# Self-attention in a hybrid decoder step: the sums of all query blocks' squares in one run of column-group passes

## The chip, the cores and the metric

The kernel runs on one core of one Trainium2 chip. The metric is the device time of one execution in microseconds. The kernel before was timed at 1400.28, 1399.35 and 1399.48 us, a median of 1399.48 us. Lower is better.

## The reference, cut to what matters

One layer of a decoder computes, for 256 prompt tokens and 8 sample tokens, a combined input projection, sliding-window attention beside a state-space (SSD) mixer, an output projection, cross-attention into 256 memory tokens, and a gated feed-forward part. The change lies in the attention of the prompt, where each of the 16 heads of 64 numbers is normed by its own root mean square:

```python
def rms_norm(x, g):
    xf = x.astype(jnp.float32)
    y = xf * lax.rsqrt(jnp.mean(xf * xf, axis=-1, keepdims=True) + EPS)
    return (y * g.astype(jnp.float32)).astype(x.dtype)
...
    proj = rms_norm(x, w['g_mix']) @ w['w_in']
    q, k, v, z, xbc, dt_raw = jnp.split(proj, IN_SPLITS, axis=-1)
    q = rms_norm(q.reshape(b, t, N_HEADS, HEAD_DIM), w['q_norm_g'])
    k = rms_norm(k.reshape(b, t, N_KV_HEADS, HEAD_DIM), w['k_norm_g'])
```

So for every token and head the kernel needs the sum of 64 squares of the query. The kernel does not scale the queries; it applies the resulting factor to the scores, before the softmax.

## The kernel before, in words

Features lie on the 128 partitions and tokens along the free axis. Every weight matrix is streamed from memory in pieces of 128x1024 (`wraw`). ScalarE rounds a piece to a high part (`whi`, L85) and VectorE subtracts it from the original to get a low part (`wlo`, L86). TensorE then makes three passes for each product: high by high (L100), high by low activations (L101), low by high (L102). A pair of output blocks fills two PSUM banks; when it is complete VectorE takes it out with the norm factor of the token (`attn` at L409 for the queries, `u` at L734 for the convolution's inputs). Everything else that TensorE does, such as transposes, scores, sums across partitions and the SSD products, is put between these projection passes. All of it stands in one queue of TensorE that is worked off in order. The tile framework's scheduler sets the order of all engines when the kernel is built, out of the order of the code and its own estimates. `tc.issue_after(x)` adds the condition that what is issued inside comes after instruction x; `tc.high_priority()` moves work ahead.

The queries are eight blocks (j = 0 to 7) of 128 features, two heads in each, in the tile `qT` (in the trace `attn`). As each pair of blocks is ready ScalarE squares it into `qsq[j // 4]` (L611). Eight float32 matmuls (L615) then add up the squares by head. The stationary operand `nw[:, d, :]` is 32 columns wide, with two columns of ones for the two heads at places 2d and 2d + 1; it lies in the tile `zz`. Block j of half d writes to the 32 partitions from 32 j of one bank `pq` (in the trace `s`), so that the four j use the four column groups of 32 of the array, and the two halves d add into the same place. The trace shows each float32 matmul as two passes, so these are 16 passes. VectorE copies the bank to `qn` (L628), TensorE transposes it (two transposes, L278, to the tile `x`), ScalarE takes the root (L634) and VectorE the reciprocal (L635). The factors `rqs` and `nrqs` enter the softmax of `attn_first` and `attn_prompt`.

The scores of the first 128 tokens are L570, those of the second L529 and L530; the transposes of the probabilities are L278 to the tile `t`; their products with the values are L597 and L559. The SSD part that follows uses L798 (`s`), L825 (`y`, eight matmuls of 64 columns, or 16 passes), L833 and L841.

Of the kernel before, what the change touches and what calls it, by code (L numbers as in the profile page):

```python
# [16 lines left out]
TP, TS = 256, 8  # L17
# [30 lines left out]
def hybrid_decoder_step_kernel(ctx: ExitStack, tc: tile.TileContext, I, O):  # L48
    nc = tc.nc
    V, S, P, PE = nc.vector, nc.scalar, nc.gpsimd, nc.tensor  # L50
# [9 lines left out]
    def psum(tag):  # L60
        return ps.tile([128, 512], F32, tag=tag, name=tag, bufs=banks[tag])

    def T3(pool, n, dt=F32, tag=None, name=None, bufs=None):
        return pool.tile([128, n, T], dt, tag=tag, name=name or tag, bufs=bufs)
# [536 lines left out]
    qsq = [T3(apool, 4, tag="R", name=f"qsq{i}", bufs=4) for i in range(2)]  # L601
    nw = zz[:, :, 512:544]
# [7 lines left out]

            S.activation(out=qsq[j // 4][:, j % 4, :TP], in_=qT[:, j, :TP], func=AF.Square)  # L611
    pq = psum("s")
    for d in range(2):
        for j in range(4):
            PE.matmul(pq[32 * j:32 * j + 32, 0:TP], nw[:, d, :], qsq[d][:, j, :TP], start=d == 0, stop=d == 1)  # L615
    cpc = mp.tile([128, 24, 8], F32, name="cpc")
    ctmp = mp.tile([128, 2, TP], F32, tag="c", name="ctmp", bufs=2).rearrange("p a b -> p (a b)")[:, :192].rearrange("p (a b) -> p a b", b=8)

# [10 lines left out]
    pq = psum("x")  # L629
# [30 lines left out]
    for j in range(8):  # L660
        if j % 4 == 0:
            second_chunk(j // 4)
        d = 2 * (j // 4)
# [893 lines left out]
def build(shapes):  # L1557

    import concourse.bacc as bacc

    nc = bacc.Bacc("TRN2", target_bir_lowering=False, num_devices=1)
    ins = {n: nc.dram_tensor(f"in_{n}_dram", s, dt, kind="ExternalInput").ap() for n, (s, dt) in shapes.items()}
    outs = {n: nc.dram_tensor(f"out_{n}_dram", s, F32, kind="ExternalOutput").ap() for n, s in _OUTS}
    with tile.TileContext(nc, schedule_with_timeline_sim=True) as tc:
        hybrid_decoder_step_kernel(tc, ins, outs)
    return nc
# [10 lines left out]
```

## Time and profile before

| what | value |
|---|---|
| median of 3 runs | 1399.48 us |
| the profiled execution's own time | 1399.1 us |
| its span, first to last instruction | 1396.8 us |
| TensorE busy | 1391.8 us of the span |
| VectorE busy | 1051.1 us |
| ScalarE busy | 769.2 us |
| DMA queue of the weights | 60.9% of 16 engines |

The profiled execution lies 0.38 us under the median; 2.3 us of it lie outside the span. In the views, "PE" is TensorE, "DVE" VectorE, "ACT" ScalarE. A row of the chain of waits has a start, the time that this piece added to the chain, the engine, the tile written and the line, and a count of passes. A row of the timeline has start, duration, engine, line, operation and tiles; a matmul's duration there contains the time in which the next one already runs, so differences of starts are used for matmuls. A bracket at the end of a row is idle time before it and what ended it.

### The profile page before, as it was taken

The numbers are of one execution on the slowest core, as the hardware profiler recorded it, in microseconds if no ns is written. First come the engines' busy times: TensorE is split into PE (matmuls) and PEld (weight loads), VectorE is DVE, ScalarE is ACT, GpSimd is POOL, SyncE is SP. The second block draws the span as 40 slices with busy tenths as digits, with TensorE's granted clock in tenths as the row PEclk, the third lists the DMA queues.
The fourth block names the chain that finished last, engine by engine and source line by source line (L and its number), as shares of the span: only waits on it lengthen the run. The fifth ranks groups of instructions, "written<-read, shape, count | busy, mean of one in ns | idle before, by whom it ended". The sixth has DMA issues, their size and how long they took to land.

```text
span 1396.8 us, 29012 instructions
## 1 busy us (share of the span) xinstructions
PE 1391.8 (100%) x11535; PEld 1366.9 (98%) x11535; DVE 1051.1 (75%) x1874; ACT 769.2 (55%) x1255; POOL 95.9 (7%) x286
## 2 busy tenths in 40 slices
PE   9999999999999999999999999999999999999999
PEld 8999999999999999899999999999999999999998
DVE  8879799999997774578777775777577757765654
ACT  7667756556545554566565544554455445543532
POOL 0000011121010000002010000000000000000000
PEclk9999999999999999999999999999999999999999
DMA  7954477777776577675676765676566656655654
GB/s 302 321 162 137 137 218 245 231 242 249 244 220 236 182 240 264 206 249 187 190 254 216 253 210 187 212 248 217 183 212 240 196 183 197 196 181 182 191 184 138
DMA packets 89479, 298.33 MB, mean 214 GB/s; under 512 B 12032, under 2 KB 17152, under 8 KB 88832
## 3 DMA queue, kind: packets, MB, share of 16 engines
q1 hardware_dynamic: 83696, 277.35, 60.9%
q0 software_dynamic: 5504, 18.88, 4.1%
q8 instruction: 90, 1.47, 0.4%
q14 instruction: 45, 0.37, 0.1%
q10 hardware_dynamic: 144, 0.26, 0.1%
HBM read 280.77 MB, written 16.23 MB: 213 GB/s over the span
## 4 chain that ended last, share of the span: by engine, by line
PE 99%; DMA 0%; ACT 0%; DVE 0%; issue 0%
PE mm L100 21%; PE mm L101 21%; PE mm L102 21%; PE t L100 10%; PE t L102 10%; PE t L101 10%; PE t L240 1%; PE y L825 1%; PE t L278 1%; PE y L841 0%; PE mm L240 0%; PE s L240 0%; PE x L278 0%; PE t L559 0%; PE x L1137 0%; DMA open<-in_open_x_dram 0%
## 5 line engine op out<-in xcount | busy, mean ns | idle before, releaser
L85 ACT CAST whi<-wraw 128x1024 fp32r<-128x1024 f32 x440 | 459.7, 1048 | 527.4 <-PE mm L101 277.7
L86 DVE TENSOR_TENSOR wlo<-wraw,whi 128x1024 fp32r<-128x1024 f32 x440 | 540.1, 1229 | 220.6 <-ACT whi L85 216.7
L100 PE MATMUL mm<-x2h,whi 128*128 128x264 f32 x704 | 199.9, 284 | 0.0
L100 PE MATMUL t<-x2h,whi 128*128 128x264 f32 x704 | 199.8, 284 | 0.0
L102 PE MATMUL t<-x2h,wlo 128*128 128x264 f32 x704 | 199.7, 284 | 0.0
L101 PE MATMUL mm<-x2l,whi 128*128 128x264 f32 x704 | 199.6, 284 | 0.0
L101 PE MATMUL t<-x2l,whi 128*128 128x264 f32 x704 | 199.5, 283 | 0.0
L102 PE MATMUL mm<-x2h,wlo 128*128 128x264 f32 x704 | 199.4, 283 | 0.0
L101 PE MATMUL mm<-hl,whi 128*128 128x264 f32 x704 | 198.7, 283 | 0.0
L102 PE MATMUL mm<-hh,wlo 128*128 128x264 f32 x704 | 198.2, 283 | 0.0
L100 PE MATMUL mm<-hh,whi 128*128 128x264 f32 x704 | 197.2, 284 | 0.0
L100 PE MATMUL mm<-xh,whi 128*128 128x264 f32 x576 | 164.7, 287 | 0.0
L101 PE MATMUL mm<-xl,whi 128*128 128x264 f32 x576 | 164.5, 287 | 0.0
L102 PE MATMUL mm<-xh,wlo 128*128 128x264 f32 x576 | 162.8, 287 | 0.0
L101 PEld LDWEIGHTS mm<-x2l,whi 128*128 128x128 f32 x704 | 132.5, 188 | 0.0
L101 PEld LDWEIGHTS t<-x2l,whi 128*128 128x128 f32 x704 | 132.5, 188 | 0.0
L100 PEld LDWEIGHTS t<-x2h,whi 128*128 128x128 f32 x704 | 132.5, 188 | 0.0
L100 PEld LDWEIGHTS mm<-x2h,whi 128*128 128x128 f32 x704 | 132.4, 188 | 0.1
L101 PEld LDWEIGHTS mm<-hl,whi 128*128 128x128 f32 x704 | 132.4, 188 | 0.0
L102 PEld LDWEIGHTS t<-x2h,wlo 128*128 128x128 f32 x704 | 132.2, 188 | 0.0
L102 PEld LDWEIGHTS mm<-x2h,wlo 128*128 128x128 f32 x704 | 132.1, 188 | 0.0
L102 PEld LDWEIGHTS mm<-hh,wlo 128*128 128x128 f32 x704 | 131.9, 188 | 0.0
(506 smaller groups left out, 2951.5 us busy)
## 6 DMA issues: line engine op xcount, KB each, us to landing
wraw<-in_w_up_dram SPq DMA_DIRECT2D x176, 512.0 KB, 4.4
wraw<-in_w_in_dram SPq DMA_DIRECT2D x96, 512.0 KB, 4.7
wraw<-in_w_dn_dram SPq DMA_DIRECT2D x88, 512.0 KB, 4.2
wraw<-in_w_out_dram SPq DMA_DIRECT2D x48, 512.0 KB, 4.3
h<-in_h_dram POOLq DMA_DIRECT2D x32, 256.0 KB, 4.7
hn<-in_h_dram SPq DMA_DIRECT2D x16, 512.0 KB, 5.0
out_state_s_dram<-hn POOLq DMA_DIRECT2D x16, 512.0 KB, 3.8
e<-dram_la SPq DMA_DIRECT2D x16, 256.0 KB, 5.1
```

The source lines that it names most:

```text
L85: S.copy(out=hi, in_=x)
L86: V.tensor_tensor(out=lo, in0=x, in1=hi.bitcast(F32), op=ALU.subtract)
L100: PE.matmul(out, wh, xh, start=start, stop=False)
L101: PE.matmul(out, wh, xl, start=False, stop=False)
L102: return PE.matmul(out, wl, xh, start=False, stop=stop)
L240: PE.matmul(first[c][:, :T], pre[k // 2][i][:, k % 2, c * 128:(c + 1) * 128], A[k // 8][x][:, k % 8, :], start=k + i + x == 0, stop=k == K ...
L278: return PE.transpose(out, in_, cst[0:k, C_ID:C_ID + k])
L825: PE.matmul(y[o:o + 64, (h // 2) * 128:(h // 2) * 128 + 128], xdt[:, h, :], es[h // 4][:, h % 4, :], start=True, stop=True)
```

## The change

The eight sums become calls of a small function. The last block of the second half, d = 1 and j = 3, is called first, and all seven others are held behind it by `issue_after`. The order of the halves is turned round: d = 1 now starts the sum and d = 0 ends it. The eight matmuls, their operands and their result are the same.

```diff
     pq = psum("s")
-    for d in range(2):
-        for j in range(4):
-            PE.matmul(pq[32 * j:32 * j + 32, 0:TP], nw[:, d, :], qsq[d][:, j, :TP], start=d == 0, stop=d == 1)
+
+    def q_sums(d, j):
+        return PE.matmul(pq[32 * j:32 * j + 32, 0:TP], nw[:, d, :], qsq[d][:, j, :TP], start=d == 1, stop=d == 0)
+
+
+    with tc.issue_after(q_sums(1, 3).ins):
+        for d in (1, 0):
+            for j in range(4 if d == 0 else 3):
+                q_sums(d, j)
     cpc = mp.tile([128, 24, 8], F32, name="cpc")
```

The scheduler makes a new order out of this. On TensorE the sums stood in three places; this is the queue before (`qsq_676` is the half d = 0, `qsq_677` is d = 1, `mm` a bank of the projection):

```order
L102 MATMUL mm<-xh_76,wlo 128x264
L615 MATMUL s<-qsq_676,zz 32x256 x4
L615 MATMUL s<-qsq_677,zz 32x256 x2
L100 MATMUL mm<-xh_74,whi 128x264
L101 MATMUL mm<-xl_75,whi 128x264
L102 MATMUL mm<-xh_74,wlo 128x264
L100 MATMUL mm<-xh_74,whi 128x264
L101 MATMUL mm<-xl_75,whi 128x264
L102 MATMUL mm<-xh_74,wlo 128x264
L100 MATMUL mm<-xh_74,whi 128x264
L101 MATMUL mm<-xl_75,whi 128x264
L615 MATMUL s<-qsq_677,zz 32x256
```

The eighth sum follows 14 projection matmuls later. Now the queue has them in one place, 33 rows of projection later than the first of them stood:

```order
L100 MATMUL mm<-xh_74,whi 128x264
L101 MATMUL mm<-xl_75,whi 128x264
L102 MATMUL mm<-xh_74,wlo 128x264
L615 MATMUL s<-qsq_677,zz 32x256 x4
L615 MATMUL s<-qsq_676,zz 32x256 x4
```

The three runs (six matmuls, one, one) have become one run of eight; the place of the last sum in the queue is about the same.

On VectorE the copy of the sums to `qn` stood right behind the low parts of the queries (`qs`):

```order
L500 COPY u_656<-x 32x256
L656 TENSOR_TENSOR qs_1094<-attn,qs_1094 64x4x128 x2
L628 COPY qn<-s 128x256
L86 TENSOR_TENSOR wlo<-wraw,whi 128x1024
L573 TENSOR_TENSOR pe<-s,cst 128x512
```

Now one subtraction of a weight piece stands ahead of it (line numbers behind the change are higher by 6: L634 is the old L628):

```order
L500 COPY u_656<-x 32x256
L662 TENSOR_TENSOR qs_1094<-attn,qs_1094 64x4x128 x2
L86 TENSOR_TENSOR wlo<-wraw,whi 128x1024
L634 COPY qn<-s 128x256
L86 TENSOR_TENSOR wlo<-wraw,whi 128x1024
```

The copy has moved behind one instruction that does not need the sums.

The new order reaches further than the sums: TensorE's queue differs in many small places up to the output projection, where the attention's and the SSD part's matmuls slide by a few to some tens of rows against the projection. One such place is the SSD product `y` (L825) of the third group's second chunk. Before, its eight matmuls were one run:

```order
L100 MATMUL t_4507<-xh0_74,whi_4517 128x264
L101 MATMUL t_4507<-xl0_75,whi_4517 128x264
L825 MATMUL y_3762<-e_3737,xdt_3758 64x128 x4
L825 MATMUL y_3762<-e_3745,xdt_3758 64x128 x4
L102 MATMUL t_4507<-xh0_74,wlo_4518 128x264
```

Now three projection matmuls stand in its middle (L831 is the old L825, L804 the old L798):

```order
L100 MATMUL t_4508<-xh0_74,whi_4511 128x264
L831 MATMUL y_3762<-e_3737,xdt_3758 64x128 x4
L102 MATMUL mm_4363<-xh1_76,wlo_4434 128x264
L100 MATMUL mm_4363<-xh1_76,whi_4433 128x264
L101 MATMUL mm_4363<-xl1_77,whi_4433 128x264
L831 MATMUL y_3762<-e_3745,xdt_3758 64x128 x4
L804 MATMUL s_3972<-CT_1574,BT_1573 128x128
```

One run of eight matmuls has become two runs of four. Of the eight such products one was in two runs before, and two are now.

## Prediction, made before the changed kernel was run

> **What bounds the kernel now.** I read the page first, its busy shares and the chain that ended last, and then TensorE's waits.
>
> ```profile
> span 1396.8 us, 29012 instructions
> ...
> PE 1391.8 (100%) x11535; PEld 1366.9 (98%) x11535; DVE 1051.1 (75%) x1874; ACT 769.2 (55%) x1255; POOL 95.9 (7%) x286
> ...
> PEclk9999999999999999999999999999999999999999
> ...
> PE 99%; DMA 0%; ACT 0%; DVE 0%; issue 0%
> ...
> PE x L201 <- DVE eps L274: 1.2, 1, 1.2
> PE t L240 <- ACT xh L161: 0.5, 1, 0.5
> ```
>
> TensorE is busy in 1391.8 of 1396.8 us, its granted clock stays in the top tenth, and 99% of the chain is its own work. The last two rows are the whole answer to the question for whom TensorE waited: 1.7 us in the kernel, both in its opening. Behind that it runs from its queue without a stop to the end. So the time is the sum of what the queue's pieces cost TensorE, and a change in that sum reaches the end in full, as long as no wait appears. The price list is the chain of waits around the sums, where the second column is what each piece added:
>
> ```profile
> 81.35 0.12 PE mm L101
> 81.47 0.12 PE mm L102
> 81.59 0.99 PE s L615 x12
> 82.58 0.32 PE mm L100
> 82.90 0.12 PE mm L101
> ...
> 83.63 0.12 PE mm L101
> 83.76 0.55 PE s L615 x2
> 84.31 0.32 PE mm L102
> 84.62 0.12 PE mm L100
> ...
> 86.20 0.12 PE mm L101
> 86.32 0.55 PE s L615 x2
> 86.87 0.32 PE mm L102
> 87.19 0.12 PE mm L100
> ```
>
> A projection pass costs 0.12 us, but the first one behind a run of sums costs 0.32. So every run pays 0.20 us on top of its own time, for the way back to the full array: 1.19 us for the twelve passes, and 0.75 us for each of the two runs of two. The three together cost 1.19 + 0.75 + 0.75 = 2.69 us. Two passes are nearly as dear as twelve, because two passes of one matmul use one column group and come one after the other.
>
> **The sums in one run.** How the price grows with the passes is in other runs of column groups, of the same 256 columns and the same width of 32:
>
> ```profile
> 551.39 0.57 PE y L1091 x8
> 551.96 0.32 PE mm L100
> ...
> 552.75 1.85 PE x L1137 x28
> ```
>
> Eight passes, four matmuls in four column groups, cost 0.57 us, no more than two passes (0.55). The four groups work at the same time. Twenty-eight passes are three and a half sets of four matmuls and cost 1.85. If a half-filled set costs as much as a full one, four sets cost 1.85 and one 0.57, and a set adds (1.85 - 0.57) / 3 = 0.43 us. Two sets then cost 0.57 + 0.43 = 1.00, which is what the twelve passes above take, one and a half sets: 0.99. So the second set is paid already, and its empty half costs nothing to fill. The sixteen passes should take 0.99 + 0.20 = 1.19 us. Lower bound: that value, since four more passes can't make it shorter. Upper bound: eight passes twice with nothing shared, 2 x (0.57 + 0.20) = 1.54. I take 1.19, the row of the same line. This part is worth 2.69 - 1.19 = 1.50 us, and 1.15 us by the upper bound.
>
> A rule speaks against this. The Trainium skill, "TensorEngine Tiling (Array Packing)", section "Performance Considerations", has an overhead of some 60 cycles on each matmul. Sixteen passes would pay it sixteen times in any order, and joining them would save nothing of it. The rows above don't show it here: six more passes in other column groups cost 0.57 - 0.55 = 0.02 us. By the rule alone the first term would be nothing instead of 1.50, and the sum would come to a loss of 0.34, the next term.
>
> **What slides along.** The order shows that the rest of the moved work is the same matmuls in other places of the same queue, so only the number and the size of the runs count. A run of full-width passes between projection passes costs no way back, for it needs no other split of the array:
>
> ```profile
> 328.01 0.22 PE s L798 x2
> 328.23 0.13 PE t L100
> ...
> 329.46 1.02 PE y L825 x16
> 330.48 0.32 PE t L102
> ...
> 372.14 0.59 PE y L825 x8
> ...
> 376.31 0.59 PE y L825 x8
> ```
>
> The pass behind L798 takes 0.13. So for the full-width pieces (L278, L529, L570, L798, L833, L841) it doesn't matter where they stand. The runs with 64 columns (L559, L597, L825) do pay the 0.20 us. Their number I counted through the new order: L559 and L597 keep one run each, L825 has one more, the split shown above. The product as one run costs 1.02 + 0.20 = 1.22 us, in two runs 2 x (0.59 + 0.20) = 1.58. I took the difference from the starts of the timeline, which have the third digit, as 0.34 us; the rounded rows here give 0.36. Lower bound of this term: nothing, if the three projection passes between the halves leave something to share; upper bound 0.36.
>
> The other engines do the same instructions as before in another order. Behind the opening TensorE waits for none of them, as the two waits above show; what they could cost is a new wait of TensorE, and that is a rival. The weights' DMAs hang on the buffers that TensorE and the splits release, and they slide with them.
>
> **The sum.** 1.50 saved and 0.34 lost make 1.16 us less. The profiled execution took 1399.1 us and would take 1397.9. It lies 0.38 us under the median of the runs, 1399.48, and I forecast the median: 1399.48 - 1.16 = 1398.3 us. By the bounds of the two terms the gain lies between 1.15 - 0.36 = 0.79 and 1.50, so 1398.0 to 1398.7. A measurement of this kernel can tell about 0.2% from no change, 2.8 us, so this is "the same" for it.
>
> **The rivals.** *The copy of the sums comes late.* VectorE now does a subtraction of a weight piece first, and the transposes of `qn` stand some 25 projection passes behind the sums, as before:
>
> ```profile
> 84.35 1.41 DVE L656 TENSOR_TENSOR qs<-attn,qs 64x512 fp32r<-64x512 f32 x2
> ...
> 86.91 0.42 DVE L628 COPY qn<-s 128x256 f32<-128x256 f32 x1 [1.16 <-PE s L615]
> 87.48 1.23 DVE L86 TENSOR_TENSOR wlo<-wraw,whi 128x1024 fp32r<-128x1024 f32 x1
> ...
> 89.83 0.38 PE L278 MATMUL x<-cst,qn 128*128 128x128 f32 x2
> ```
>
> The copy ends at 86.91 + 0.42 = 87.33, and the transposes start at 89.83: 2.50 us to spare. A subtraction ahead of it costs at most 1.23 us, and VectorE stood idle for 1.16 us there, so it may well fit into that. Even the whole 1.23 leaves 1.27 us, and TensorE doesn't wait. It would begin to wait if the copy were late by more than 2.50 us, and the change would be a loss from 2.50 + 1.16 = 3.66 us on. The same section of the skill's page on tiling says that the copy out of PSUM can become the bottleneck when column groups make TensorE faster. Here the copy has to end before a fixed place in the queue, and by these rows it does. Chance 2%, at 1400 us.
>
> *The eviction of a convolution block comes late: the kernel gets slower.* From 96 us on the attention's VectorE work lies between the subtractions and the evictions that hand a bank back to the projection, and the new order shifts it by some 3 us against these. The tightest place that I found:
>
> ```profile
> 80.00:120.00 40.00, 40.00 (x318) 36.53 (x317) 32.33 (x81) 30.37 (x73) 0.00 (x0) 1.00 0.46 137
> ...
> 200.00:240.00 40.00, 40.00 (x342) 38.89 (x341) 40.00 (x78) 20.31 (x36) 5.24 (x10) 1.00 0.78 248
> ...
> 179.33 0.43 DVE L734 TENSOR_TENSOR u<-mm,r 128x264 f32<-128x264 f32 x1
> ...
> 180.10 0.28 PE L100 MATMUL mm<-xh,whi 128*128 128x264 f32 x1
> ```
>
> In the first two rows VectorE (third pair) is busy in 32.33 of 40 us, later in all 40: work that comes late isn't caught up quickly. In the last two the eviction ends at 179.76, and the pass that needs the bank starts at 180.10, 0.34 us later. One subtraction of 1.23 us ahead of such an eviction costs TensorE 1.23 - 0.34 = 0.89 us. One of these leaves a gain of 0.27; two make 0.62 us of loss, 1400.1; three 1.51, 1401.0; five 3.29, over 0.2%. For it speaks how full VectorE is; against it that it left TensorE no wait at all in the order before, made by the same scheduler. Chance of two to four 5%, of five or more 2%.
>
> *A gap elsewhere takes the gain.* If a wait of about 1 us appears in one place, or the opening is a little longer, the time is 1399.2 to 1399.6. Nothing in the rows speaks for one place above another. Chance 10%.
>
> *Only the sums count.* If the split of L825 costs nothing, the gain is 1.50: 1398.0. Chance 8%.
>
> *More than 0.2% faster.* This takes 1.6 us beyond the sum, and TensorE has no waits that could be removed. Chance 2%. That the change doesn't do what it says is excluded by the order shown above.
>
> **How the numbers follow.** The forecast, a gain of 0.8 to 1.4, has the remaining 71%. The likeliest median is 1398.3 us. The range takes in the bounds, the cases without a gain and the scatter of the runs before (1399.35 to 1400.28): 1397.4 to 1399.8. It leaves out the losses of two late evictions and more, and gains of over 2 us. Faster by over 0.2% has 2%, slower by over 0.2% 2%, the rest is 96%.
>
> **What would show it.** In the new profile's chain of waits there should be one row of L615 with sixteen passes, at 85 to 86 us, near 0.99 us, followed by a projection pass of 0.32. The products L825 should show four rows of eight passes at 0.59 and six of sixteen at 1.02, where one was split before. TensorE's waits should stay at the two of the opening. The forecast is wrong if the row of sixteen costs 1.3 us or more, if TensorE's waits name VectorE or ScalarE between 85 and 410 us, or if the span shrinks by less than 0.8 or more than 1.6 us.

## The result, and the profile after

The changed kernel takes 1404.08 us, the median of six runs (1402.73 to 1405.7), against 1399.58 us for the kernel before in six runs beside them (1399.32 to 1400.28). The ratio is 1.0032, with an interval of 1.0022 to 1.0043. So the change costs 4.5 us, where a gain of 1.16 was forecast. The profiled execution of the changed kernel took 1402.73 us, the shortest of its six. Further down, medians and ratios leave out three executions that were far longer than all others of their kernel: 1684 and 4834 us in e6 and 5864 us in e11.

These are the page of the changed kernel and its waits of TensorE.

```profile
span 1400.7 us, 29014 instructions
...
PE 1392.5 (99%) x11535; PEld 1367.8 (98%) x11535; DVE 1053.3 (75%) x1874; ACT 767.8 (55%) x1255; POOL 91.5 (7%) x286
...
PE 95%; DVE 3%; issue 1%; DMA 1%; ACT 0%; SPq 0%; DVEq 0%
```

```profile
PE y L831 <- ACT hp L849: 3.4, 1, 3.4
...
PE t L100 <- DVE u L896: 0.2, 1, 0.2
```

The span has grown from 1396.8 to 1400.7 us. TensorE is busy for nearly as long as before (1392.5 against 1391.8 us), but it has a wait that it did not have: 3.4 us, once, at the SSD product L831 (the old L825), for ScalarE's copy L849 (the old L843). The chain, 99% TensorE before, is now 95%.

The sums themselves went as forecast. The chain of waits of the changed kernel around them:

```profile
85.20 1.00 PE s L615 x16
86.20 0.33 PE mm L100
86.53 0.12 PE mm L101
```

One row of sixteen passes, 1.00 us, and 0.33 - 0.12 = 0.21 us for the way back: 1.21 in place of 2.69 us, a gain of 1.48.

**The wait.** First the kernel before, its timelines of TensorE and of ScalarE at this place (fourth group, first chunk):

```profile
368.19 1.02 PE L841 MATMUL y<-xw,Bn 128*128 128x512 f32 x2
...
372.07 0.66 PE L825 MATMUL y<-e,xdt 128*64 128x128 f32 x8
```

```profile
369.25 0.59 ACT L843 COPY hp<-y 128x512 f32<-128x512 f32 x1 [0.17 <-PE y L841]
```

The state product L841 fills a bank `y`, ScalarE copies it to `hp`, and the next product L825 fills a bank `y` again. There is one buffer for this name, so L825 may begin only when the copy has ended. It ended at 369.25 + 0.59 = 369.84, and L825 came at 372.07: 2.23 us to spare. The same place in the changed kernel, TensorE and then ScalarE:

```profile
364.26 1.02 PE L847 MATMUL y<-xw,Bn 128*128 128x512 f32 x2
368.67 0.66 PE L831 MATMUL y<-e,xdt 128*64 128x128 f32 x8 [3.39 <-ACT hp L849]
```

```profile
359.53 1.28 ACT L815 ACTIVATE e<-e,la 128x128 f32<-128x128 f32 x4 [3.52 <-DMA e<-dram_la]
...
362.74 2.04 ACT L93 CAST ath<-attn 128x1056 fp32r<-128x1056 f32 x2
364.68 1.05 ACT L85 CAST whi<-wraw 128x1024 fp32r<-128x1024 f32 x1
365.62 0.63 ACT L816 ACTIVATE e<-e 128x512 f32<-128x512 f32 x1
366.16 1.98 ACT L85 CAST whi<-wraw 128x1024 fp32r<-128x1024 f32 x2
368.04 0.58 ACT L849 COPY hp<-y 128x512 f32<-128x512 f32 x1
```

The two users of the bank now stand next to each other on TensorE, and the product is there as soon as the state product ends. ScalarE works its own queue off in order: two casts of `ath`, a cast of `whi`, an exponential, two more casts, and only then the copy. It is late with all of them: ahead of them it had stood for 3.52 us for the load of `e`. In the kernel before it was idle when the state product ended (the bracket at L843). TensorE stands for 3.39 us.

This wait has two parts. L847 ended at 364.26 + 1.02 = 365.28 us and the copy began at 368.04, so some 2.8 us of it are ScalarE's lateness, and only about 0.6 are the copy itself. By an estimate from these rows, neighbours with a free ScalarE would have cost about 0.6 us. And the old distance, 2.86 us from the end of L841 (369.21) to L825, would not have quite hidden a copy that ends 3.34 us behind the state product. No run separates the two parts, and that the load of `e` made ScalarE late is read from its queue alone.

The adjacency can be read from the new order of TensorE, without any time:

```
L100 MATMUL mm_4987<-ath_4981,whi_4991 128x264
L100 MATMUL mm_4988<-ath_4981,whi_4991 128x264
L847 MATMUL y_4013<-xw_3998,Bn_2135 128x512
L831 MATMUL y_4044<-e_4019,xdt_4040 64x128 x4
L101 MATMUL mm_4987<-atl_4982,whi_4991 128x264
```

In the order before, 24 rows of projection stood between these two, and nowhere in it did a new user of a bank `x`, `y` or `s` stand fewer than 21 matmuls behind the last writer of the one before.

**What follows the wait.** The chain behind it in the changed kernel, and a table of windows (busy time of TensorE, weight loads, VectorE, ScalarE and GpSimd, then the granted clock):

```profile
369.33 0.42 PE mm L101
369.75 0.22 PE mm L102
...
372.61 0.22 PE mm L101
372.83 0.17 PE mm L102
```

```profile
370.00:373.00 3.00, 3.00 (x16) 3.00 (x16) 3.00 (x6) 0.87 (x3) 0.54 (x1) 0.53 0.63 197
373.00:376.00 3.00, 3.00 (x26) 3.00 (x26) 3.00 (x6) 1.05 (x1) 0.00 (x0) 1.00 0.97 285
```

For 3.5 us after the wait a projection pass costs 0.22 instead of 0.12 us; the clock granted between 370 and 373 us is 0.53, and then again 1.00. Fourteen passes (369.75 to 372.61) at 0.10 more, and the two at the ends, are 1.5 us.

So the two traces differ by: sums -1.48; the further split of L831 +0.35; the wait +3.5 (TensorE's idle 3.39, and the overlap of the next pass that is lost); the slow passes +1.5; a stall of 0.2 us for VectorE at 297.32, with what is lost around it +0.45; the opening -0.35. Together +4.0 us, and the spans differ by 3.9.

### The profile page after: what moved, and what is told of

It reads as the page before. It is cut to its first block, busy times and chain, and to the rows that moved or that the text cites. A ratio compares the mean times of both kernels' runs of the same rounds, so it can differ in the third digit from the quotient of the medians.

```text
span 1400.7 us, 29014 instructions
## 1 busy us (share of the span) xinstructions
PE 1392.5 (99%) x11535; PEld 1367.8 (98%) x11535; DVE 1053.3 (75%) x1874; ACT 767.8 (55%) x1255; POOL 91.5 (7%) x286
## 3 DMA queue, kind: packets, MB, share of 16 engines
q8 instruction: 90, 1.47, 0.4%
## 4 chain that ended last, share of the span: by engine, by line
PE 95%; DVE 3%; issue 1%; DMA 1%; ACT 0%; SPq 0%; DVEq 0%
PE mm L100 20%; PE mm L101 20%; PE mm L102 20%; PE t L100 9%; PE t L101 9%; PE t L102 9%; DVE wlo L86 1%; PE t L240 1%; DVE c L751 1%; PE t L278 1%; PE y L831 0%; PE s L240 0%; PE mm L240 0%; DMA open<-in_open_dram 0%; PE t L559 0%
```

## The experiments

The theory was that the adjacency in the bank `y` costs the time, as the wait and its slow passes. The rival was that VectorE is what the kernel runs up against between 200 and 380 us, and that a TensorE which comes earlier merely waits for it, in this place or others. Ratios are to the kernel before, run beside each experiment (medians 1399.29 to 1399.42).

**e1: the changed kernel again.** No edit.

> The changed kernel once more, for the scatter and a second trace. Bank theory: TensorE again waits once, in front of the SSD product of the last group, for ScalarE's copy of the state out of the one bank y (3.4 us in the first trace), and runs some 15 passes at 0.22 us behind it; where the time is longer than the 1402.73 us of the first trace, this wait is longer by about as much. Time 1402.5 to 1405.7. Late-splits theory (VectorE's low parts of the attention output and of the weights are late there in any order): the same time, and the longer run shows longer waits for VectorE instead. Sixteen passes in one run: 1.2 us with the way back.

Measured: 1404.49 us (1403.55 to 1405.7), ratio 1.0035, interval 1.0022 to 1.0048. Its profiled execution was a long one, 1405.70 us, and its waits of TensorE are:

```profile
PE y L831 <- ACT hp L849: 3.1, 1, 3.1
...
PE x L278 <- DVE xw L826: 0.5, 1, 0.5
PE mm L100 <- DVE u L740: 0.4, 1, 0.4
PE t L100 <- DVE u L896: 0.4, 1, 0.4
```

The wait at the bank comes again, no longer than in the shorter execution. Between the two spans lie 3.1 us. Most of them are the further waits for VectorE (1.3 us in place of 0.2), a longer stretch of slow passes (20 at 0.22 us, with the product itself at 1.12 in place of 0.66: some 1.1 us) and an opening longer by 0.7. So the bank is not all of it.

**e2 and e12: the state product in another bank.** The changed kernel, with the state product of this one place in the bank `x`; e12 is the same kernel on another chip.

```diff
-            st = psum("y")
+            st = psum("x" if (g, c) == (3, 0) else "y")
```

> The state product of the last group's first chunk goes to the bank x in place of y, so the SSD product that follows in the queue needs no copy out of its bank; the projection passes and the splits behind it stay at the same place. Bank theory: the wait of 3.4 us and the slow passes behind it (15 x 0.10 = 1.5 us) go, and at most 0.6 us remain for the low part of the attention output, which came at 366.4 in the first trace: 1397.6 to 1399.2 us. Late-splits theory: TensorE only waits one instruction later for VectorE, and the time stays at 1402 to 1405 us.

> The changed kernel with the state product in the bank x once more, for a second trace, since its runs lay between 1399.75 and 1404.27 us and its first trace was the fastest of them. Late-VectorE theory: where this trace is of a slower run, TensorE waits longer for VectorE at places where the first trace shows waits of 0.2 to 0.4 us (205, 299 and 370 us), and passes at 0.22 us follow where a wait is over 2 us. Time 1400 to 1404 us.

Measured: e2 1402.1 us (1399.75 to 1404.27), ratio 1.0019, interval 1.001 to 1.0028; e12 1401.02 us (1399.65 to 1402.03), ratio 1.0012, interval 1.0003 to 1.0021. The edit did more than change the bank: in e2's trace the state product starts at 354.31 us in place of 364.26, and the product L831 that stood next to it at 366.76. So it takes away the neighbours together with the shared bank. The wait at `y` and the slow passes are gone from both traces, and e2's median is 2.4 us under e1's, beside which it ran. A loss of 2.8 (e2) and 1.6 us (e12) is left against the kernel before. The waits of e2's execution (1399.75 us, its shortest), and then of e12's (1401.85 us):

```profile
PE t L100 <- DVE u L896: 0.4, 1, 0.4
PE mm L102 <- DVE wlo L86: 0.2, 1, 0.2
PE mm L100 <- DVE u L740: 0.2, 1, 0.2
```

```profile
PE mm L101 <- DVE atl L93: 0.9, 2, 0.6
PE mm L102 <- DVE wlo L86: 0.6, 1, 0.6
PE mm L100 <- DVE u L740: 0.5, 1, 0.5
PE t L100 <- DVE u L896: 0.5, 1, 0.5
```

Every new wait is for VectorE: 0.8 us in the shorter execution, 2.5 in the longer, which makes 1.7 of the 2.1 us between them. Both theories hold a part.

**e3: the copy made twice.** The changed kernel, with a second copy of the same bank on ScalarE.

```diff
                 S.copy(out=hp, in_=st)
+                if g == 3:
+                    S.copy(out=hp, in_=st)
```

> ScalarE copies the state of the last group's first chunk twice out of the bank, which adds one copy of 128x512, 0.5 us, ahead of the release of the bank and nothing else. Bank theory: TensorE's wait grows by 0.5 us, and the time is 0.4 to 0.8 us above the changed kernel of this call. Late-splits theory: no change, within 0.2 us.

Measured: 1404.57 us (1404.42 to 1404.78), ratio 1.0038, interval 1.0024 to 1.0052. Its timelines of TensorE and of ScalarE:

```profile
370.39 0.77 PE L831 MATMUL y<-e,xdt 128*64 128x128 f32 x8 [4.06 <-ACT hp L851]
```

```profile
369.15 0.57 ACT L849 COPY hp<-y 128x512 f32<-128x512 f32 x1
369.76 0.59 ACT L851 COPY hp<-y 128x512 f32<-128x512 f32 x1
```

The wait is 4.06 us instead of 3.39 and 3.1, longer by 0.7 to 1.0 us, about a copy with what lies around it: it ends when ScalarE has copied. The median hardly moved against e1's (by 0.08 us, with ranges that overlap), so the time by itself shows nothing here.

**e4: how long a standstill makes the passes slow.** The kernel before, and behind its last output eight stretches: 80 projection-like passes, then a chain of n copies on ScalarE that TensorE has to wait for, then the next 80.

```diff
...
+    for n in (2, 4, 5, 6, 7, 8, 10, 14):
+        lp = psum("mm")
+        for i in range(80):
+            PE.matmul(lp[:, :T], lx[:, 0, 0:128], lx[:, 1, :], start=i == 0, stop=i == 79)
+        S.activation(out=lt[0], in_=lp[:, :T], func=AF.Copy, scale=0.0)
+        for i in range(n - 2):
+            S.copy(out=lt[(i + 1) % 2], in_=lt[i % 2])
+        S.copy(out=lx[:, 1, :], in_=lt[n % 2])
...
```

> The kernel before, and behind its last output a ladder that computes nothing of use: eight times 80 passes of 264 columns, each followed by a chain of 2, 4, 5, 6, 7, 8, 10 and 14 ScalarE copies of 128x264 (some 0.43 us each) on which the next 80 passes wait. It measures from which idle time on TensorE's passes come at 0.22 us in place of 0.12, and for how long. If the slow passes of the changed kernel come from its idle time, they show behind idle times of 3.4 us and more, for about 3 us, and not behind the shortest (0.9 us); if they come from something else in that place, all batches run at 0.12 us. The total is some 100 us above the kernel before and is not compared.

Measured in one execution. Its chain of waits, the rows of 80 passes of which five are shown (the idle time ahead of a row is its start less the end of the one before it):

```profile
1404.95 10.05 PE mm L1425 x80
...
1416.86 10.05 PE mm L1425 x80
...
1429.21 11.56 PE mm L1425 x80
...
1458.21 11.36 PE mm L1425 x80
...
1473.14 10.05 PE mm L1425 x80
```

After 0.9 and 1.9 us of standstill the 80 passes cost 10.05 us. After 2.3, 2.7, 3.2, 4.5 and 6.3 us they cost 1.3 to 1.5 us more, and the surplus does not grow with the standstill. After 3.6 us it was absent once; the last section shows why. So the 1.5 us behind the wait in the changed kernel come from the wait: there 3.5 us of standstill cost 5.0.

**e5: the kernel before with the state product in the other bank.** The edit of e2, without the change.

```diff
-            st = psum("y")
+            st = psum("x" if (g, c) == (3, 0) else "y")
```

> The control for the kernel with the state product in the bank x: the same move of that one product, in the kernel before. If the move itself costs nothing, 1398.8 to 1399.8 us, as the kernel before. If the move is what cost the 2 to 3 us that were left there, 1401 us or more. What is left of the loss then belongs to the new order (late VectorE theory) in the first case, and to the experiment in the second.

Measured: 1399.06 us (1398.4 to 1399.36), ratio 0.9998, interval 0.9989 to 1.0006; TensorE waits in the opening alone. The state product moved here as well, from 368.19 to 354.65 us. The move to another bank costs nothing, so the loss that e2 keeps belongs to the new order.

**e6 and e7: the changed kernel and the kernel before with less for VectorE.** Both leave out `ssd_sample`, the sample's part of the state work, and its loads.

```diff
     ych = mp.tile([128, KB, 8], F32, name="ych")
+    P.memset(ych, 0.0)
 
     def ssd_sample(g):
+        if g in (0, 1, 2, 3):
+            return
```

> The changed kernel without the 32 products and 32 sums that VectorE makes for the sample's state and their loads (the sample's part of the SSD output is then wrong): some 44 us of VectorE's work between 180 and 420 us is gone. In the order that results no product of the single banks stands closer than 21 rows to the one before, and every SSD product is one run. Late-VectorE theory with the bank theory: TensorE has no waits left behind the opening, the change shows its price list alone, and the time is 1.5 us below the same kernel with the sums in three runs: 1397.0 to 1398.5 us. Theory that the run of sixteen or the order of the sums itself costs time: it stays above that kernel by 2 us or more.

> The kernel before without the same 64 VectorE instructions and their loads; every SSD product is one run here as well, where one was split before. All theories: no waits of TensorE, 0.3 us less than the kernel before for the one split less, 1398.5 to 1399.7 us. The difference to the lean changed kernel is the price of the three runs of sums against one: 1.5 us by the price list.

Measured: e6 (with the change) 1397.4 us, ratio 0.9987, interval 0.9978 to 0.9996; e7 (without it) 1399.58 us (1398.59 to 1400.47), ratio 1.0002, interval 0.9993 to 1.001. With the change it is 2.2 us shorter. In both orders the product of 64 columns is eight unbroken runs, with no neighbours in a bank, so that in TensorE's own work the sums are all that differs. First the windows of the changed kernel, then those of e6:

```profile
200.00:380.00 180.00, 176.39 (x1453) 169.39 (x1453) 178.24 (x344) 102.98 (x184) 25.80 (x39) 0.99 0.75 238
```

```profile
200.00:380.00 180.00, 179.78 (x1496) 173.19 (x1495) 155.63 (x314) 108.54 (x198) 11.02 (x8) 1.00 0.62 198
```

VectorE (third pair) is busy for 178.24 of 180 us in the changed kernel and for 155.63 in e6. Where it has room, the gain of the sums comes through. The edit takes out loads and work of GpSimd too (DMA share 0.75 to 0.62, GpSimd 25.80 to 11.02 us), so the room on VectorE is not all that differs from the changed kernel; e6 and e7 share all that. The spans differ by 1398.1 - 1395.7 = 2.4 us: 1.48 for the sums, and 0.9 because two short waits of e7 (1.1 us for VectorE's `xs`) are one of 0.2 in e6.

**e8: the copy on VectorE.** The changed kernel, where VectorE makes the copy of this group. The new order has no neighbours in `y`, and the last product is one run again.

```diff
-                S.copy(out=hp, in_=st)
+                if g == 3:
+                    V.tensor_copy(out=hp, in_=st)
+                else:
+                    S.copy(out=hp, in_=st)
```

> VectorE in place of ScalarE copies the state of the last group out of the bank. The scheduler then puts no two users of the bank y next to each other (21 rows between them at least). Bank theory alone: no wait of 3 us and no slow passes, 1397.8 to 1399.2 us. With late VectorE as the second cause: better than the changed kernel by 2 us or more, but with short waits for VectorE's evictions at some 205 and 297 us and a scatter of over 2 us: 1399.5 to 1402.5 us.

Measured: 1399.99 us (1398.69 to 1401.11), ratio 1.0005, interval 0.9996 to 1.0013, level with the kernel before, where e1 has 1.0035. Of the forecast gain nothing is left, and its waits say where it went:

```profile
PE mm L100 <- DVE u L740: 1.3, 1, 1.3
...
PE mm L101 <- DVE atl L93: 0.4, 1, 0.4
```

The first one, 1.3 us, is for the eviction of a convolution block, at 205.9 us.

**e9, e10 and e11: neighbours without the change, and the change without neighbours.** In e9 the copies to `cnew` are moved to GpSimd in the kernel before; its new order happens to set the same two users of `y` next to each other. In e10 the copies to `zsam` go too, and they stand 23 rows apart in the trace. e11 has both edits in the changed kernel, and no neighbours.

```diff
-            V.tensor_copy(out=cnew[:, bi, :], in_=u[:, TP:])
+            P.tensor_copy(out=cnew[:, bi, :], in_=u[:, TP:])
...
-            V.tensor_copy(out=zsam[:, 2 * i + m, :], in_=z[:, TP:])
+            P.tensor_copy(out=zsam[:, 2 * i + m, :], in_=z[:, TP:])
```

> The kernel before, with its sums in three runs, but with the 24 small copies of convolution state made by GpSimd in place of VectorE. This takes work from VectorE and would help it; but in the order that the scheduler makes of it the SSD product of the last group stands right behind the state product in the bank y, as in the changed kernel. Bank theory: TensorE waits there some 2 to 4 us for ScalarE's copy and runs passes at 0.22 us behind it: 1401.5 to 1404.5 us, though the sums are not touched. Theory that the loss belongs to the run of sixteen, or to a late VectorE alone: as the kernel before or a little faster, 1398.5 to 1399.8 us.

> As the one above, and the 16 small copies of z go to GpSimd as well. In this order the two users of the bank y are 21 rows or more apart. Bank theory: no wait there, 1398.5 to 1399.8 us, 2 us or more under the one above. If the copies on GpSimd are what costs time, this one is slow too.

> The changed kernel with the same 40 small copies on GpSimd: sums in one run, no adjacent users of a single bank, two SSD products in two runs. Bank theory with late VectorE: the price list gives 1.50 - 0.34 = 1.16 us under the kernel before, less what TensorE still waits for VectorE: 1397.8 to 1399.5 us, 3 us or more under the changed kernel. If the run of sixteen costs something that the price list doesn't show, 1401 us or more.

Measured: e9 1407.99 us (1405.67 to 1411.16), ratio 1.0064, interval 1.005 to 1.0078; e10 1405.31 us (1402.26 to 1406.73), ratio 1.0037, interval 1.0024 to 1.0051; e11 1401.0 us, ratio 1.0011, interval 1.0002 to 1.002. The waits of e9 and then of e10:

```profile
PE y L825 <- ACT hp L843: 2.3, 1, 2.3
PE mm L100 <- ACT whi L85: 1.7, 1, 1.7
```

```profile
PE mm L102 <- DVE wlo L86: 2.5, 4, 1.1
PE mm L100 <- ACT whi L85: 1.9, 1, 1.9
```

The wait at `y` is there without the sums' change, as soon as the order has the neighbours, and it is absent where they stand apart: the order makes it, not the sums. By the times the three are a poor test. e10 was expected near the kernel before and is 6 us over it, from waits of another kind that the edits brought; e9 ended 3.5 us over the top of its range, and e11 1.5 us over its own. e11, with the change, is 4.3 us shorter than e10, which is more than the sums explain. Each edit makes a new order, and each order has waits of its own.

**e13 and e14: the sample's work later.** e8 and e2, each with `ssd_sample(0)` behind `ssd_prompt(1)`, to take VectorE's work on the state `h` away from 205 us.

```diff
-    ssd_sample(0)
     ssd_prompt(1)
+    ssd_sample(0)
```

> The changed kernel with VectorE copying the last group's state out of the bank (no adjacent users of the bank) and with the first quarter of the sample's state work one SSD product later, so that VectorE doesn't stand behind the loads of that work at 196 to 207 us. If these loads are what makes VectorE late there, the wait at some 206 us goes and with it the scatter: 0.5 to 1.5 us under the kernel with VectorE's copy alone (1399.99), 1398.3 to 1399.5 us. If VectorE is late from its fullness in any order, 1399.5 to 1401 us, with the wait somewhere else.

> The same move of the sample's work in the kernel with the state product in the bank x, whose two calls gave 1402.1 and 1401.02 us. If the loads make VectorE late, its wait at 206 us goes, those at 299 and 370 us may stay: 1399.5 to 1400.8 us. If VectorE is late from its fullness, 1401 to 1402 us as before.

Measured: e13 1399.81 us (1399.16 to 1401.25), ratio 1.0004, interval 0.9995 to 1.0013; e14 1400.92 us (1399.5 to 1404.25), ratio 1.0013, interval 1.0004 to 1.0022. They are level with e8 and with e12. The wait of 1.3 us at 205.9 in e8 is gone from e13's trace, but the median shows no gain that can be told from none. In these traces VectorE still stands around 205 us for loads of `h` and `cb` (1.1 and 0.3 us in e13). Whether it is late there because of the loads or because it is full is not settled. No version that computes everything was faster than the kernel before by more than its interval.

## Why the prediction was wrong, point by point

**The price of the sums** held: 1.00 + 0.21 measured, 0.99 + 0.20 forecast. The empty half of the second set of column groups was paid already. One sentence of the prediction does not fit the rows beside it: two passes (0.55 us) are as dear as eight (0.57), and not nearly as dear as twelve (0.99). No term used it. The rule of the Trainium skill that was weighed against it ("TensorEngine Tiling (Array Packing)", "Performance Considerations": about 60 cycles of overhead for each matmul) does not show in the row: four more passes than the run of twelve added 0.01 us.

**The further split of L825** held. The chain of the changed kernel has four rows of eight passes. The two halves at 321.73 and 322.88 are 0.59 each, and each pays for a way back; that is 0.35 us more than one run, where 0.34 was forecast.

**The step that failed** is this one: "for the full-width pieces (L278, L529, L570, L798, L833, L841) it doesn't matter where they stand". It is right for what a piece costs TensorE, and wrong for what it needs. L841 and L825 write to the same single bank, with a copy by ScalarE between them. How far apart they stand, and how far behind ScalarE is at that moment, decide whether that copy is hidden. The old order had 24 rows there and 2.23 us to spare; the new one has no row there, and a ScalarE that is 2.8 us late. The wait of 3.39 us and the 1.5 us of slow passes behind it are the term that the sum put at nothing. The sentence before the rivals, that the other engines "do the same instructions as before in another order" and that a wait would be a rival, had the right question; but the only places searched were the copy of the sums and VectorE's evictions. ScalarE's copies out of a bank were not looked at, and the pair of rows could have been found in the new order.

**The copy of the sums comes late** (2%): it did not. In the changed kernel it ends at 86.97 us and the transposes start at 89.27, so 2.30 us are left. What the Trainium skill ("TensorEngine Tiling (Array Packing)", "Performance Considerations") is cited for there, a copy out of PSUM that becomes the bottleneck when column groups make TensorE faster, no run shows: the copy that TensorE waited for is that of a full-width product, and it was late because it had no cover left and stood behind other work of ScalarE.

**An eviction of a convolution block comes late** (7%): this was the second cause, and its chance was too small. The timelines of both engines in the kernel before and in the changed one, around the same eviction:

```profile
205.88 0.43 DVE L734 TENSOR_TENSOR u<-mm,r 128x264 f32<-128x264 f32 x1
...
207.16 0.28 PE L100 MATMUL mm<-xh,whi 128*128 128x264 f32 x1
```

```profile
204.74 0.43 DVE L740 TENSOR_TENSOR u<-mm,r 128x264 f32<-128x264 f32 x1
...
205.34 0.28 PE L100 MATMUL mm<-xh,whi 128*128 128x264 f32 x1
```

Before, the eviction ended at 206.31 and its bank was needed at 207.16: 0.85 us to spare. Now it ends at 205.17 and the bank is needed at 205.34: 0.17. TensorE comes 1.82 us earlier and VectorE only 1.14. The prediction argued that VectorE left no wait in the order before. But the change makes TensorE earlier by 1.5 us against an engine that is busy in 175.26 of 180 us there and cannot come earlier by as much. In the changed kernel's shortest execution such waits cost 0.2 us, in e1 1.3. Where the wait at `y` is removed (e2, e8, e12), waits for VectorE take the gain; with room on VectorE (e6 against e7) it arrives. That VectorE is the limit is shown by the waits, and the scatter of the executions follows them (e2 against e12); the exact share of each of its stalls is not.

**The gap elsewhere** (10%) was put at about 1 us. The wait was 3.5, and brought 1.5 more with it that no term held.

**The signs** named in the prediction did their work: the sum row and the rows of L825 are as forecast, and the waits name ScalarE and VectorE between 85 and 410 us, which was said to prove it wrong.

## What to carry to other kernels

When a change makes a new order, list for every buffer that exists once how far the last writer of one use and the first of the next stand apart in their queue, whose copy lies between, and what stands ahead of that copy in its own queue; a list of prices holds only as long as none of these handovers has lost its cover. Here a gain on the busiest engine was worth no more than the slack of the next full one, read at the places where they hand over. A standstill of TensorE can cost 1.5 us more than it lasts, and in e1 some 2.6; in these traces it did where it left TensorE less than about 1.5 us of work in one of the windows of 3.41 us described below.

## What the runs showed of the hardware

A projection pass that costs 0.12 us costs 0.22 after a standstill, in the changed kernel from 369.40 to 372.81 us, for 3.41 us, at a granted clock of 0.50. In the ladder of e4 it came after 2.3 us and more (five times in six) and not after 0.9 and 1.9; in e9 a wait of 2.31 us had no such passes behind it. The Trainium skill, "TensorE: Matmul & The Clock Gate", section "Part 1: The HAM clock gate", has the clock fall to a half after an idle window of about 3.4 us, and rise again after as much work, with windows that run freely. The length of the slow stretch and the clock agree with that; the standstill that is enough was shorter here, 2.3 us.

The traces also show why the length of the standstill does not decide by itself. The times at which the clock switches lie whole multiples of 3.41 us apart within a trace (in e4 at 1430.43, 1433.85, 1444.09, 1447.50 us and so on), so each trace can be cut into windows of this length that do not follow the work. These are the window of the standstill of 2.3 us in e4 and the one behind it, and then the two windows that share the standstill of 3.6 us:

```profile
1427.02:1430.43 3.41, 1.22 (x10) 1.23 (x11) 0.00 (x0) 2.01 (x5) 0.00 (x0) 1.00 0.00 0
1430.43:1433.85 3.42, 3.42 (x18) 3.42 (x17) 0.00 (x0) 0.00 (x0) 0.00 (x0) 0.50 0.00 0
...
1467.98:1471.40 3.42, 1.58 (x13) 1.36 (x12) 0.00 (x0) 1.68 (x5) 0.00 (x0) 1.00 0.00 0
1471.40:1474.81 3.41, 1.67 (x13) 1.67 (x14) 0.00 (x0) 1.59 (x4) 0.00 (x0) 1.00 0.00 0
```

After a window with 1.22 us of work on TensorE the clock is 0.50 in the next. The longer standstill lies across two windows, leaves 1.58 and 1.67 us of work in them, and the clock stays at 1.00. The window of e9's wait (369.61 to 373.02 us) has 1.75 us of work, and its clock stays too. In e1 the first slow window (369.64 to 373.05 us) held part of the wait and 2.47 us of work, the next was slow as well, and the slow stretch lasted 6.83 us. In all traces of this case the clock fell behind every full-speed window with up to 1.47 us of work (nine inside the kernels, and the ends of the executions besides) and behind none with 1.55 or more.

Runs of column-group passes, 32 wide and of 256 columns, are charged by sets and not by number: two passes cost 0.55 us, eight 0.57, twelve 0.99 and sixteen 1.00, each run with about 0.20 us for the way back to the full array.
